# Hybrid decoder layer: the causal mask of the stick-breaking heads, as matrix products or as zeros written by GpSimd

## The chip, the cores and the metric

One core of a Trainium2 chip runs the whole layer. The metric is the device time in microseconds (us) of one execution; several executions are timed and the median is given. One further execution is recorded by the hardware profiler, and all trace times below are of that one.

## The reference

The layer reads 256 tokens of width 1024. One input projection feeds 8 heads of stick-breaking attention and 8 heads of dilated-window softmax attention; both are normalised per head, joined, projected, added to the input, layer-normed, and followed by a SwiGLU feed-forward network (width 2816) with a second layer norm. Only the stick-breaking part is changed:

```python
def stick_breaking_attention(q, k, v):
    ...
        z = jnp.einsum('bhqd,bhkd->bhqk', q_blk, k).astype(jnp.float32) * scale
        mask = key_pos[None, :] < q_pos[:, None]
        log_stay = jnp.where(mask, jax.nn.log_sigmoid(-z), 0.0)
        after = lax.cumsum(log_stay, axis=3, reverse=True) - log_stay
        w = jnp.where(mask, jnp.exp(jax.nn.log_sigmoid(z) + after), 0.0)
        return jnp.einsum('bhqk,bhkd->bhqd', w.astype(v.dtype), v)
```

A query sees only keys strictly before it. Outside of the mask, the softplus of the score counts as zero in the cumulative sum, and the weight is zero.

## The kernel before

Products that need accuracy are made of two fp32r parts, a rounded one ("hi") and the rest ("lo"): `prod` (L223) issues three TensorE products, hi by hi, hi by lo, lo by hi. So every weight must be split before use. `split` (L78) does that with an ACT copy into `whi` and a DVE subtraction into `wlo`. The class `Weights` (L82) loads chunks of 128x2048 over the SP queue into `wraw` and splits them piece by piece, 512 columns at a time.

Heads go in pairs, `j` = 0 to 3 stick-breaking, 4 to 7 dilated. A stick-breaking pair passes these steps:

- `evacuate` (L253) copies a pair's projected queries and keys out of PSUM in hi and lo parts: `padhi` on ACT and `padlo` on DVE for each head, then `oh` on ACT and `ol` on DVE.
- `stick_scores` (L280), step 1, makes the scores, transposed (keys on the partitions): `z0` (128x512: two heads, first block of keys against all 256 queries) and `z1` (128x256: second block of keys against the second block of queries). Two more products with `identb` as weights and the bf16 tile `maskb` (zeros, and -1e30 where a key isn't before its query) add the mask to the four diagonal blocks. Then ACT computes Abs, Exp and Ln into `ab`, DVE completes the softplus (L300, one instruction for each of `z0` and `z1`), rounds it to `sph` (L301) and subtracts for `spl` (L302).
- `stick_weights` (L305), step 2, adds the cumulative sums to the scores with six products (L311), and ACT takes Exp into `w0` and `w1` (L314, L315).
- `values` (L363), step 3, multiplies with the values (L370, L375) and squares; `normalise` (L384), step 4, sums the squares with `blkr` (L388) and scales.

TensorE's order of these steps among the projection's products is laid out by the class `Order` (L408). It keeps a clock, `now`, in its own units. `fill(cost, fn)` first runs every step that is due, then issues one group of projection products and adds its cost to `now`: 0.65 for three 512-column products of the value projection (`v_proj`, L468), 0.33 for three 256-column ones (`qk_proj`, L484). A step that runs adds its own cost, and the next step of its pair falls due its lag later. `LAG_A` (L29) holds the lags from evacuation to step 1, to step 2, to step 3 and to step 4. Step 3 also waits until the value projection is out (`v_at`). The first two pairs are special: their projections come before the loop, and `attend` is called at `now` = 0 with lags 0.65 and 3.1. In the kernel before:

```python
    attend(0, p01[0], 0.65)
    ...
    attend(1, p01[1], 3.1)
    ...
        od.after(lags[0] if lag is None else lag, 1.2 if a_kind else 0.97, step1)
```

Behind them come the value projection of the stick-breaking heads (16 fills, chunks 0 and 1), the query-key projections of pairs 2 and 3, the value projection of the dilated heads, and so on. All eight pieces of chunks 0 and 1 are issued ahead of the first fill: one, then the evacuation of pair 0, two more, the evacuation of pair 1, and five more.

The framework's scheduler may move instructions of an engine past each other by its own estimate of when they are ready. The wrapper `Pinned` (L62) holds the instructions issued through it (`prod`, `split`, `evacuate`) in program order, up to step 1 of pair 1; from there on it is off. ACT's and DVE's instructions of `stick_scores` are not issued through it.

Of the kernel before, what the change touches and what calls it, by code (L numbers as in the profile page):

```python
# [12 lines left out]
BF16 = mybir.dt.bfloat16  # L13
AF = mybir.ActivationFunctionType
ALU = mybir.AluOpType
# [10 lines left out]

PACE = 1.39
LEAD = 5
LAG_A = (5.13, 7.73, 1.37, 1.88)  # L29
LAG_B = (3.34, 5.0, 1.13, 4.28)  # L30
LAG_LN = 5.92
LAG_LN1 = 5.94
# [11 lines left out]
NEG = -1.0e30  # L44
# [3 lines left out]
def decoder_layer(ctx: ExitStack, tc: tile.TileContext, first, x, wqk, wv, wo, wgu, wd,  # L48
                  gmix, lnrows, biases, out):
    nc = tc.nc  # L50
    cst = ctx.enter_context(tc.tile_pool(name="cst", bufs=1))
# [21 lines left out]
    pe, act_e, dve = Pinned(nc.tensor), Pinned(nc.scalar), Pinned(nc.vector)  # L73

    def bank(tag, name):
        return ps.tile([128, 512], F32, tag=tag, name=name)
# [112 lines left out]
    negones = cst.tile([128, 128], F32R, name="negones")  # L189
    negtri = cst.tile([128, 128], F32R, name="negtri")  # L190
    ident = cst.tile([128, 128], F32, name="ident")
    identb = cst.tile([128, 128], BF16, name="identb")
    maskb = cst.tile([128, 128], BF16, name="maskb")
    blkr = cst.tile([128, 128], F32R, name="blkr")
    along, back = [[1, 128]], [[-1, 128]]

    nc.gpsimd.memset(maskb, 0.0)
    nc.gpsimd.affine_select(maskb, maskb, along, ALU.is_gt, NEG, base=0, channel_multiplier=-1)
    nc.gpsimd.memset(ident, 1.0)
    nc.gpsimd.affine_select(ident, ident, back, ALU.is_equal, 0.0, base=0, channel_multiplier=1)  # L200
    nc.gpsimd.tensor_copy(identb, ident)
    nc.gpsimd.memset(negones.bitcast(F32), -1.0)
    nc.gpsimd.affine_select(negtri, negones.bitcast(F32), back, ALU.is_ge, 0.0, base=0, channel_multiplier=1)
    nc.gpsimd.memset(blkr.bitcast(F32), 0.0)
# [18 lines left out]
    def prod(dst, lhs, rhs, start, stop):  # L223

        pe.matmul(dst, lhs[0], rhs[0], start=start, stop=False, skip_group_check=True)
        pe.matmul(dst, lhs[0], rhs[1], start=False, stop=False, skip_group_check=True)
        pe.matmul(dst, lhs[1], rhs[0], start=False, stop=stop, skip_group_check=True)
# [25 lines left out]
    def evacuate(j, p):  # L253

        a_kind = j < 4
        ph, pl = padded[j % 2]
        oh = at.tile([128, S], F32R, tag="oh", name="oh")
        ol = at.tile([128, S], F32R, tag="ol", name="ol")
        qs = slice(0, 256)
        ks = slice(256, 512)  # L260
        pc, oc = (qs, ks) if a_kind else (ks, qs)
        pscale, oscale = (SCALE, 1.0) if a_kind else (1.0, SCALE)
        for h in range(2):
            r = slice(h * 64, h * 64 + 64)
            c = slice(h * 256, h * 256 + 256)
            act_e.activation(ph[r, c], p[r, pc], AF.Copy, scale=pscale)
            dve.scalar_tensor_tensor(pl[r, c], p[r, pc], pscale, ph[r, c],
                                     op0=ALU.mult, op1=ALU.subtract)
        act_e.activation(oh, p[:, oc], AF.Copy, scale=oscale)
        dve.scalar_tensor_tensor(ol, p[:, oc], oscale, oh, op0=ALU.mult, op1=ALU.subtract)  # L270
        return (ph, pl), (oh, ol)

    def heads(t, n):
        return t[:, :2 * n].rearrange("p (h n) -> p h n", h=2)

    def second(t):

        return t.rearrange("p (h n) -> p h n", h=2)[:, :, 128:256]

    def stick_scores(j, pad, plain):  # L280
        ph, pl = pad
        oh, ol = plain
        z0 = bank("big", "z0")
        z1 = bank("sml", "z1")
        prod(z0, (oh[:, 0:128], ol[:, 0:128]), (ph, pl), True, True)
        prod(heads(z1, 128), (oh[:, 128:256], ol[:, 128:256]), (second(ph), second(pl)), True, True)
        mb = maskb[:, None, :].to_broadcast([128, 2, 128])
        z0d = z0.rearrange("p (h n) -> p h n", h=2)
        pe.matmul(z0d[:, :, 0:128], identb, mb, start=False, stop=True, skip_group_check=True)
        pe.matmul(heads(z1, 128), identb, mb, start=False, stop=True, skip_group_check=True)  # L290
        sph = sk.tile([128, 768], F32R, tag="sph", name="sph")
        spl = sk.tile([128, 768], F32R, tag="spl", name="spl")
        ab = at.tile([128, 768], F32, tag="ab", name="ab")
        parts = ((z0, slice(0, 512), 512), (z1, slice(512, 768), 256))
        for z, c, n in parts:
            nc.scalar.activation(ab[:, c], z[:, :n], AF.Abs)
        nc.scalar.activation(ab, ab, AF.Exp, scale=-1.0)
        nc.scalar.activation(ab, ab, AF.Ln, bias=1.0)
        for z, c, n in parts:
            nc.vector.scalar_tensor_tensor(ab[:, c], z[:, :n], 0.0, ab[:, c], op0=ALU.max, op1=ALU.add)  # L300
        nc.vector.tensor_copy(sph, ab)  # L301
        nc.vector.tensor_sub(spl, ab, sph)  # L302
        return z0, z1, sph, spl

    def stick_weights(z0, z1, sph, spl):  # L305
        z0d = z0.rearrange("p (h n) -> p h n", h=2)
        for sp in (sph, spl):
            s1 = sp[:, 512:768]
            for dst, lhs, rhs in ((z0, negtri, sp[:, 0:512]), (z0d[:, :, 128:256], negones, heads(s1, 128)),
                                  (z1[:, :256], negtri, s1)):  # L310
                nc.tensor.matmul(dst, lhs, rhs, start=False, stop=True, skip_group_check=True)  # L311
        w0 = at.tile([128, 512], F32, tag="w0", name="w0")
        w1 = at.tile([128, 256], F32, tag="w1", name="w1")
        nc.scalar.activation(w0, z0, AF.Exp)  # L314
        nc.scalar.activation(w1, z1[:, :256], AF.Exp)  # L315
        return w0, w1

    bias_sb = at.tile([128, 8, 256], F32, name="bias_sb", bufs=1)
# [124 lines left out]
    od = Order()  # L443

    def attend(j, p, lag=None):

        a_kind = j < 4
        pad, plain = evacuate(j, p)
        scores, weigh = (stick_scores, stick_weights) if a_kind else (dilated_scores, dilated_weights)
        lags = LAG_A if a_kind else LAG_B  # L450

        def step1():
            x1 = scores(j, pad, plain)
            Pinned.on = Pinned.on and j == 0

            def step2():
                x2 = weigh(*x1)

                def step3():
                    x3 = values(j, *x2)  # L460
                    od.after(lags[3], 0.43, lambda: normalise(j, *x3))
                od.after(lags[2], 0.68, step3, lambda: v_at.get(j // 4, 1e9) <= od.now)
            od.after(lags[1], 0.9 if a_kind else 0.65, step2)
        od.after(lags[0] if lag is None else lag, 1.2 if a_kind else 0.97, step1)

    vt, v_at = {}, {}

# [16 lines left out]
    def qk_proj(j, c0):  # L484
        w = weights.get(c0)
        p = bank("in", "p_in")
        for half in range(2):
            for kt in range(KT):
                od.fill(0.33, lambda: qk_step(p, w, half, kt, kt == 0))
        weights.free(c0)  # L490
        attend(j, p)


    weights.piece(512)
    attend(0, p01[0], 0.65)
    for _ in range(2):
        weights.piece(512)
# [213 lines left out]
    base = 14 + NFF  # L711
# [117 lines left out]
```

## Time and profile before

| | us |
|---|---|
| median of 3 runs (317.07 to 317.55) | 317.19 |
| the profiled execution | 316.86 |
| its span, first to last instruction | 315.1 |
| TensorE busy in the span | 305.9 |
| VectorE (DVE) busy | 240.6 |
| ScalarE (ACT) busy | 190.7 |
| GpSimd (POOL) busy | 4.1 |

The profiled execution took 1.76 us more than its span, which lie around it, and it is 0.33 us under the median. In the rows below, PE is TensorE's products and PEld its weight loads. Products overlap in the pipeline and the ends shown for them are modelled, so what a product costs is read from one start to the next, not from its duration. A row of the timeline gives its start, its duration, the instruction, how many were merged, and in brackets the engine's idle time before it with what ended it.

### The profile page before, as it was taken

The numbers are of one execution on the slowest core, as the hardware profiler recorded it, in microseconds if no ns is written. First come the engines' busy times: TensorE is split into PE (matmuls) and PEld (weight loads), VectorE is DVE, ScalarE is ACT, GpSimd is POOL, SyncE is SP. The second block draws the span as 40 slices with busy tenths as digits, with TensorE's granted clock in tenths as the row PEclk, the third lists the DMA queues.
The fourth block names the chain that finished last, engine by engine and source line by source line (L and its number), as shares of the span: only waits on it lengthen the run. The fifth ranks groups of instructions, "written<-read, shape, count | busy, mean of one in ns | idle before, by whom it ended". The sixth has DMA issues, their size and how long they took to land.

```text
span 315.1 us, 5440 instructions
## 1 busy us (share of the span) xinstructions
PE 305.9 (97%) x2112; PEld 277.8 (88%) x2112; DVE 240.6 (76%) x465; ACT 190.7 (61%) x406; POOL 4.1 (1%) x22
## 2 busy tenths in 40 slices
PE   8999999999999999999999999999999999999990
PEld 4988898799997778999999999999999988888880
DVE  4778998659897479997646466585597699999765
ACT  5789997777787458666446364473542675565011
POOL 5000000000000000000000000000000000000000
PEclk9999999999999999999999999999999999999998
DMA  7979887297332104789455464563613253630011
GB/s 255 399 301 381 277 283 263 113 358 292 151 137 69 64 2 133 249 294 370 157 189 214 139 226 172 166 235 133 218 50 136 80 188 130 270 135 0 0 67 67
DMA packets 9657, 58.02 MB, mean 184 GB/s; under 512 B 1184, under 2 KB 1440, under 8 KB 3360
## 3 DMA queue, kind: packets, MB, share of 16 engines
q1 hardware_dynamic: 9344, 57.22, 49.8%
q10 hardware_dynamic: 288, 0.46, 0.4%
q8 instruction: 16, 0.26, 0.3%
q14 instruction: 9, 0.07, 0.1%
HBM read 56.63 MB, written 1.05 MB: 183 GB/s over the span
## 4 chain that ended last, share of the span: by engine, by line
PE 94%; DVE 2%; ACT 1%; DMA 1%; issue 0%; DVEq 0%
PE pg L71 40%; PE p_in L71 22%; PE d L71 15%; PE acc L71 7%; PE z L71 2%; PE o L370 1%; PE s L71 1%; PE warm L185 1%; PE z L311 1%; DVE y L563 1%; PE o L375 1%; DVE bst L548 1%; DMA out_h<-y 1%; DVE y L546 1%; PE o L388 1%; PE tr L575 1%
## 5 line engine op out<-in xcount | busy, mean ns | idle before, releaser
L71 DVE TENSOR_TENSOR wlo<-wraw,whi 128x512 fp32r<-128x512 f32 (+2 forms) x194 | 138.0, 739 | 37.9 <-ACT whi L71 37.0
L71 ACT ACTIVATE whi<-wraw 128x512 fp32r<-128x512 f32 (+2 forms) x194 | 121.2, 671 | 58.0 <-PE pg L71 35.2
L71 PE MATMUL pg<-xhi,whi 128*128 128x256 f32 x304 | 85.7, 282 | 0.0
L71 PE MATMUL pg<-xlo,whi 128*128 128x256 f32 x304 | 85.5, 281 | 0.0
L71 PE MATMUL pg<-xhi,wlo 128*128 128x256 f32 x304 | 85.5, 281 | 0.0
L71 PEld LDWEIGHTS pg<-xhi,whi 128*128 128x128 f32 x304 | 57.2, 188 | 0.0
L71 PEld LDWEIGHTS pg<-xlo,whi 128*128 128x128 f32 x304 | 57.2, 188 | 0.0
L71 PEld LDWEIGHTS pg<-xhi,wlo 128*128 128x128 f32 x304 | 57.2, 188 | 0.0
L71 PE MATMUL p_in<-xhi,whi 128*128 128x256 f32 x128 | 36.5, 286 | 0.0
L71 PE MATMUL p_in<-xhi,wlo 128*128 128x256 f32 x128 | 36.3, 283 | 0.0
L71 PE MATMUL p_in<-xlo,whi 128*128 128x256 f32 x128 | 36.1, 282 | 0.0
L71 PE MATMUL d<-whi,s 128*128 128x512 f32 x84 | 26.9, 395 | 0.0
L71 PE MATMUL d<-whi,a 128*128 128x512 f32 (+1 forms) x92 | 25.9, 363 | 0.0
L71 PEld LDWEIGHTS p_in<-xhi,whi 128*128 128x128 f32 x128 | 24.1, 188 | 1.4 <-issue 0.7
L71 PEld LDWEIGHTS p_in<-xlo,whi 128*128 128x128 f32 x128 | 24.1, 188 | 0.2
L71 PEld LDWEIGHTS p_in<-xhi,wlo 128*128 128x128 f32 x128 | 24.1, 188 | 0.1
L71 PEld LDWEIGHTS d<-whi,s 128*128 128x128 f32 x84 | 15.8, 188 | 3.8
L71 PEld LDWEIGHTS d<-whi,a 128*128 128x128 f32 x92 | 16.6, 189 | 2.9
L71 PE MATMUL d<-wlo,a 128*128 128x512 f32 (+1 forms) x46 | 16.7, 363 | 0.0
L71 PE MATMUL d<-wlo,s 128*128 128x512 f32 x42 | 16.6, 395 | 0.0
L71 ACT ACTIVATE s<-slots 128x896 fp32r<-128x896 f32 x6 | 5.7, 953 | 13.4 <-DVE slots L611 13.4
L71 PE MATMUL pg<-wlo,xhi 128*128 128x256 f32 x48 | 13.6, 286 | 0.0
(151 smaller groups left out, 473.7 us busy)
## 6 DMA issues: line engine op xcount, KB each, us to landing
wraw<-in_wgu SPq DMA_DIRECT2D x22, 1024.0 KB, 4.8
wraw<-in_wd SPq DMA_DIRECT2D x11, 1024.0 KB, 4.8
wraw<-in_wqk SPq DMA_DIRECT2D x6, 1024.0 KB, 5.7
wraw<-in_wo SPq DMA_DIRECT2D x4, 1024.0 KB, 4.7
wraw<-in_first SPq DMA_DIRECT2D x8, 384.0 KB, 6.3
wraw<-in_wv SPq DMA_DIRECT2D x3, 1024.0 KB, 5.4
rows<-in_lnrows SPq DMA_DIRECT2D x2, 1024.0 KB, 6.6
wraw<-in_wv SPq DMA_DIRECT2D x2, 512.0 KB, 7.0
```

The source lines that it names most:

```text
L71: return lambda *a, **k: tc.keep_in_program_order(f(*a, **k)) if Pinned.on else f(*a, **k)
L185: nc.tensor.matmul(warm.rearrange("p (r n) -> p r n", r=4), idle, idle[:, None, :].to_broadcast([128, 4, 128]), start=True, stop=True, ski ...
L311: nc.tensor.matmul(dst, lhs, rhs, start=False, stop=True, skip_group_check=True)
L370: nc.tensor.matmul(o[r, 0:256], vt[g, 0][:, c], w0[:, h * 256:h * 256 + 256], start=True, stop=False, skip_group_check=True)
L375: nc.tensor.matmul(o[r, 128:256], vt[g, 1][:, c], w1[:, h * 128:h * 128 + 128], start=False, stop=True, skip_group_check=True)
L388: nc.tensor.matmul(ms, blkr, sq[:, i, :], start=i == 0, stop=i == 1, skip_group_check=True)
L546: nc.vector.scalar_tensor_tensor(y[:, c], res[:, c], scale, acc[i][:, :c.stop - c.start], op0=ALU.mult, op1=ALU.add)
L548: nc.vector.bn_stats(st[:, i, :], y[:, c])
L563: nc.vector.scalar_tensor_tensor(dst[:, c], y[:, c], r[:, 3:4], b[:, c], op0=ALU.mult, op1=ALU.add)
L575: nc.tensor.transpose(p[:, i * 128:i * 128 + 128], h[:, kt * 128:kt * 128 + 128], ident)
```

## The change

The two mask products of each stick-breaking pair go, and with them `maskb` and `identb` and the three GpSimd instructions that built these. In their place a function `causal` lets GpSimd write zeros into the diagonal blocks (128 columns of each of two heads, 256 columns an instruction) of `ab` after the softplus, and of `w0` and `w1` after the exponential: four instructions for a pair, 16 in all. The second and third lag of `LAG_A` are longer, and the cost that `Order` counts for step 1 is 1.05 in place of 1.2.

```diff
-LAG_A = (5.13, 7.73, 1.37, 1.88)
+LAG_A = (5.13, 8.4, 2.1, 1.88)
...
-    identb = cst.tile([128, 128], BF16, name="identb")
-    maskb = cst.tile([128, 128], BF16, name="maskb")
...
-    nc.gpsimd.memset(maskb, 0.0)
-    nc.gpsimd.affine_select(maskb, maskb, along, ALU.is_gt, NEG, base=0, channel_multiplier=-1)
...
-    nc.gpsimd.tensor_copy(identb, ident)
...
+    def causal(t, n):
+
+        d = t.rearrange("p (h n) -> p h n", h=2)[:, :, 0:128]
+        nc.gpsimd.affine_select(d, d, [[0, 2], [1, 128]], ALU.is_gt, 0.0, base=0, channel_multiplier=-1)
+
     def stick_scores(j, pad, plain):
...
-        mb = maskb[:, None, :].to_broadcast([128, 2, 128])
-        z0d = z0.rearrange("p (h n) -> p h n", h=2)
-        pe.matmul(z0d[:, :, 0:128], identb, mb, start=False, stop=True, skip_group_check=True)
-        pe.matmul(heads(z1, 128), identb, mb, start=False, stop=True, skip_group_check=True)
...
         for z, c, n in parts:
             nc.vector.scalar_tensor_tensor(ab[:, c], z[:, :n], 0.0, ab[:, c], op0=ALU.max, op1=ALU.add)
+            causal(ab[:, c], n)
         nc.vector.tensor_copy(sph, ab)
         nc.vector.tensor_sub(spl, ab, sph)
...
         nc.scalar.activation(w0, z0, AF.Exp)
+        causal(w0, 512)
         nc.scalar.activation(w1, z1[:, :256], AF.Exp)
+        causal(w1, 256)
...
-        od.after(lags[0] if lag is None else lag, 1.2 if a_kind else 0.97, step1)
+        od.after(lags[0] if lag is None else lag, 1.05 if a_kind else 0.97, step1)
```

## Rows read from the trace of the kernel before

**Rows 1.** Page, part 1: engine, busy time (share of the span), instructions.
```profile
PE 305.9 (97%) x2112; PEld 277.8 (88%) x2112; DVE 240.6 (76%) x465; ACT 190.7 (61%) x406; POOL 4.1 (1%) x22
```

**Rows 2.** All waits of PE: who waited for whom, us in total, times, longest.
```profile
PE warm L185 <- DVE idle L182: 1.1, 1, 1.1
PE o L370 <- ACT w L359: 0.2, 1, 0.2
```

**Rows 3.** Timeline of PE, 18.8 to 23 us: step 1 of pairs 0 and 1.
```profile
18.86 0.28 PE L71 MATMUL z<-padhi,ol 128*128 128x256 f32 x1
18.98 0.39 PE L71 MATMUL z<-maskb,identb 128*128 128x256 bf16 x2
...
19.45 0.39 PE L71 MATMUL p_in<-wlo,xhi 128*128 128x512 f32 x1
...
20.60 0.47 PE L71 MATMUL z<-padhi,oh 128*128 128x512 f32 x1
...
21.91 0.48 PE L71 MATMUL p_in<-whi,xhi 128*128 128x512 f32 x1
...
22.69 0.39 PE L71 MATMUL p_in<-whi,xhi 128*128 128x512 f32 x1
```

**Rows 4.** Timeline of PE, the same passage from 256 to 512 columns without masks.
```profile
29.09 0.28 PE L311 MATMUL z<-spl,negtri 128*128 128x256 f32 x1
...
29.44 0.39 PE L71 MATMUL p_in<-wlo,xhi 128*128 128x512 f32 x1
```

**Rows 5.** Timeline of ACT, then of DVE, 18 to 27 us: evacuation of pair 1, splits.
```profile
18.78 0.38 ACT L71 ACTIVATE padhi<-p_in 64x256 fp32r<-64x256 f32 x1 [0.90 <-DVE padlo L71]
19.30 0.87 ACT L296 ACTIVATE ab<-z 128x512 f32<-128x512 f32 x2
20.06 0.39 ACT L71 ACTIVATE oh<-p_in 128x256 fp32r<-128x256 f32 x1
20.32 2.72 ACT L71 ACTIVATE whi<-wraw 128x512 fp32r<-128x512 f32 x5
...
20.48 0.42 DVE L71 SCALAR_TENSOR_TENSOR ol<-p_in,oh 128x256 fp32r<-128x256 f32 x1 [0.86 <-ACT oh L71]
21.00 3.10 DVE L71 TENSOR_TENSOR wlo<-wraw,whi 128x512 fp32r<-128x512 f32 x5
...
26.56 0.68 DVE L71 TENSOR_TENSOR wlo<-wraw,whi 128x512 fp32r<-128x512 f32 x1
```

**Rows 6.** Timeline of PE around step 3: pairs 0 and 1 together, then pair 3.
```profile
34.24 0.28 PE L71 MATMUL p_in<-xhi,wlo 128*128 128x256 f32 x1
...
36.12 0.28 PE L71 MATMUL p_in<-xlo,whi 128*128 128x256 f32 x1
...
64.64 0.28 PE L71 MATMUL p_in<-xhi,wlo 128*128 128x256 f32 x1
...
65.87 0.28 PE L71 MATMUL p_in<-xlo,whi 128*128 128x256 f32 x1
```

**Rows 7.** Timeline of POOL, whole span, three of its 22 instructions.
```profile
1.65 0.20 POOL L202 MEMSET negones<- 128x128 f32 x1
...
2.04 0.29 POOL L203 TENSOR_SCALAR_AFFINE_SELECT negtri<-negones 128x128 fp32r<-128x128 f32 x1
...
4.21 0.52 POOL L248 MEMSET padlo<- 128x512 f32 x1
```

**Rows 8.** Stretch table (busy us of PE, PEld, DVE, ACT, POOL), then DVE and PE timelines.
```profile
24.00:39.00 15.00, 15.00 (x98) 12.86 (x97) 13.96 (x25) 14.89 (x32) 0.00 (x0) 1.00 0.89 332
...
36.32 0.92 DVE L381 TENSOR_TENSOR sqh<-sq,sqh 128x256 fp32r<-128x256 f32 x2
...
37.41 0.40 PE L388 MATMUL o<-sqh,blkr 128*128 128x256 f32 x2
```

**Rows 9.** Timelines of DVE and of PE: pair 2, end of step 1, step 2.
```profile
53.73 0.96 DVE L302 TENSOR_TENSOR spl<-ab,sph 128x768 fp32r<-128x768 f32 x1
...
57.20 0.41 PE L311 MATMUL z<-spl,negtri 128*128 128x512 f32 x1
```

More of the change, by code (lines that the diff above doesn't have):

```diff
@@ L191, in decoder_layer @@
     ident = cst.tile([128, 128], F32, name="ident")
-    identb = cst.tile([128, 128], BF16, name="identb")
-    maskb = cst.tile([128, 128], BF16, name="maskb")
     blkr = cst.tile([128, 128], F32R, name="blkr")
-    along, back = [[1, 128]], [[-1, 128]]
-    nc.gpsimd.memset(maskb, 0.0)
-    nc.gpsimd.affine_select(maskb, maskb, along, ALU.is_gt, NEG, base=0, channel_multiplier=-1)
+    back = [[-1, 128]]
     nc.gpsimd.memset(ident, 1.0)
     nc.gpsimd.affine_select(ident, ident, back, ALU.is_equal, 0.0, base=0, channel_multiplier=1)
-    nc.gpsimd.tensor_copy(identb, ident)
     nc.gpsimd.memset(negones.bitcast(F32), -1.0)
```

## The prediction, made before the changed kernel was run

> **What bounds the kernel now.** I read the page's busy shares first: TensorE is busy 305.9 of 315.1 us, every other engine 76% or less [rows 1]. Then the waits of TensorE alone: in the whole span there are two, 1.1 us for the warm-up at the start and 0.2 us for a dilated pair [rows 2]. So in the stage of the stick-breaking heads, from 17 to 68 us, TensorE's products follow one another without a wait, and a change is worth what it takes out of TensorE's sequence or puts in as a wait. The third view is the timeline around each changed instruction, where I look for two things: the cost of a mask product from start to start, and how soon before its use each operand is ready.
>
> **What the masks cost.** From the last 256-column product of pair 0's scores (18.86) to the second 512-column product behind the masks (19.45) are 0.59 us [rows 3]. The same passage without masks is 29.09 to 29.44, 0.35 us [rows 4]. So the two masks of a pair cost 0.24 us (four pairs show 0.23 to 0.24), and removing eight products takes 4 x 0.24 = 0.96 us out of TensorE's sequence. If nothing else moved, that would be the gain: 0.3%.
>
> **What the new cost and lags do to the order of pair 1.** The order can be worked out from the planner's numbers. Before: the first fill ends at 0.65, step 1 of pair 0 runs and takes `now` to 1.85, two fills take it to 3.15; this is past 3.1, so step 1 of pair 1 runs ahead of the fourth fill. The trace agrees: its first product starts at 20.60, the fourth fill at 21.91 [rows 3]. After: step 1 of pair 0 counts 1.05, `now` is 1.70, after two fills 3.00. That is not 3.1. So a third fill is issued, and step 1 of pair 1 follows the fourth fill in all. Both go through the pinned wrapper, so the scheduler can't swap them back.
>
> The fourth fill multiplies with piece 3 of chunk 0, and this piece is late. ACT's and DVE's orders are pinned too: the piece stands behind the evacuation of pair 1. DVE makes `ol` from 20.48, then five splits from 21.00 [rows 5], and the first of them is this piece. One split takes 0.68 [rows 5], so it ends at 21.68. In the kernel before, the fourth fill's second product, the first that reads `wlo`, starts 0.32 after 21.91 (as 19.45 does behind its masks), at 22.23: 0.55 us of cover. After, without the first pair's masks, the fourth fill comes at 20.60 - 0.24 = 20.36, its second product at 20.59. The cover is gone.
>
> How early can the piece be? With the mask of `z0` gone, ACT's two Abs need not wait for it: they start at 19.30 where `padhi` ended at 18.78 + 0.38 = 19.16 [rows 5]. Neighbours on ACT overlap by some 0.1, so Abs gains 0.1 to 0.25, and `oh`, `ol` and the split gain the same: the piece ends at 21.43 to 21.58. TensorE follows an operand by about 0.15 (`oh` ends at 20.45, the product starts at 20.60 [rows 3, 5]). So the second product starts at 21.58 to 21.73, and with two products of 0.23 behind it step 1 of pair 1 starts at 22.04 to 22.19, though it would be due at 20.36 + 0.69 = 21.05: a new stall of 1.0 to 1.15 us. If the scheduler places the Abs after the pieces instead, `oh` comes some 0.4 earlier, and the stall is 0.7; if nothing on ACT gets earlier it is 1.25.
>
> The sum at a common point, the start of the fifth fill: before 22.69 [rows 3]. After: 22.04 to 22.19, plus three products of 0.235 and three of 0.12 (1.06), so 23.10 to 23.25. That is +0.41 to +0.56, I take +0.48, with both masks of pairs 0 and 1 already taken out (bounds with the two other placements +0.1 to +0.65). The masks of pairs 2 and 3 bring -0.48. These two cancel.
>
> **Steps 2 and 3.** By the same arithmetic, after the change steps 2 of both pairs stand one or two fills later, and step 3 of pair 0 comes one fill behind the value projection, with step 3 of pair 1 four fills later. Before, both step 3 came together. From the last product ahead to the second behind, the two together take 36.12 - 34.24 = 1.88, less two pitches of 0.12: 1.64. Pair 3 alone takes 65.87 - 64.64 = 1.23, so 0.99 [rows 6]. Two apart cost 1.98: +0.34 (range 0.2 to 0.4, since the matrix switches form four times and not twice).
>
> **GpSimd's own work.** No row shows a 256-column select. One of 128 columns took 0.29; a memset grows from 0.20 (128 columns) to 0.52 (512), 0.11 per 128 [rows 7]. So an instruction takes between 0.29 and 0.58; I take 0.40, from the memset's slope. For the softplus the first select hides under DVE's second instruction; the second delays `sph` by about 0.40 plus two handovers of 0.15, 0.7 in all; the weights are delayed by the same 0.7. Step 2 gets one fill more (0.69) and 0.67 more of lag, step 3 0.73 more. In pair 2 `spl` ended at 54.69 and was used at 57.20, 2.5 us of cover [rows 9], and so no stall there. In pairs 0 and 1 DVE and ACT have no slack: 13.96 and 14.89 of 15 us busy [rows 8]. There the new stall is 0 to 0.8; I take 0, since the fills added equal the delay and the scheduler may fill gaps with other products from there on. Below zero it doesn't go: nothing waits now. The three instructions that GpSimd saves at the start (about 0.8 us) cost and give nothing: its last one ended long before the first evacuation.
>
> Behind a waiting `sph` stand, on DVE, the splits of later weights and, from 36.32, the squares that step 4 needs. The squares ended at 37.24, and TensorE used the first at 37.41 [rows 8]; that first one ended about 36.8, 0.6 ahead.
>
> The rule that speaks against this change: the Trainium skill, "SBUF — State Buffer", section "SBUF: two separate sides", says that DVE and GpSimd share one pair of ports by an exclusive lock, held for the whole instruction by whichever starts first, for DVE instructions with two SBUF inputs as well. No row here shows it: GpSimd's last instruction comes just before DVE's first subtraction. By that rule each select among the splits would hold DVE up, or be held up; without it the sum stays as it is, and with it the result is the second rival below.
>
> **The sum.** +0.48 - 0.48 + 0.34 = +0.34 us, so 317.2 against the profiled 316.86, and against the median of 317.19 about 317.5. Its own range is -0.18 (0.1 - 0.48 + 0.2) to +1.37 (0.65 - 0.48 + 0.4 + 0.8): 317.0 to 318.6.
>
> **The rivals.** *The stall doesn't come* (0.20): the fourth fill and step 1 of pair 1 stay swapped, or the piece is split earlier than the pinned order says. Then the masks' 0.96 come out, less 0.34 for the separated step 3: 316.6; without that 316.2. For it: from 24 us on the scheduler does move products. Against it: up to 24 us the trace follows the program's order exactly.
>
> *DVE is held up by GpSimd* (0.25), which ends slower: DVE is busy without a gap from 25 us to the squares of step 4, so a delay there goes through to TensorE's products of step 4. Eight selects of pairs 0 and 1 at 0.40 make 3.2 us if every one holds DVE up. It decides once the delay exceeds the 0.6 us of cover. With half of the eight, 1.6 us, the stall is 1.0 on top of the forecast: 318.5; with all it would be 2.6, 320.1.
>
> *The forecast* has the rest, 0.55.
>
> **How the numbers follow.** A measurement can tell about 0.2%, 0.63 us, from no change: 316.56 to 317.82. Of the forecast's 0.55, most (0.42) lies inside and 0.13 above. Of the first rival 0.13 is faster and 0.07 inside. Of the second 0.20 is slower and 0.05 inside. That makes faster 0.13, same 0.54, slower 0.33. For 8 in 10 the range reaches from 316.5 (cuts off half of the first rival) to 318.6 (cuts off a part of the second).
>
> **What would show it.** Right: in the trace after, TensorE waits near 21 us for a `wlo` or `whi` (none is listed now), the fourth fill stands ahead of pair 1's scores, the fifth fill starts near 23.2, and the two step 3 stand apart. The fifth fill starting near 22.2 would show the first rival; TensorE waiting for `sqh`, `sph` or `spl` between 28 and 40 us, with GpSimd's selects or DVE's splits longer than their 0.3 to 0.6 and 0.68, the second. Wrong altogether would be a difference that arises behind 68 us, where no instruction of the change stands.

## The result and the profile after

The changed kernel takes 318.89 us (median of 5 runs, 318.6 to 319.4) against 317.32 us before: 1.57 us more, ratio 1.0052 (95% interval 1.0041 to 1.0064). It is slower by more than the 0.2% that can be told from no change, and above the predicted range (316.5 to 318.6). Its profiled execution took 319.1 us, its span is 317.4 us. In this document a median is that of all runs of a kernel, and a ratio leaves out the few runs far above the kernel's fastest (one of the five of e5 below, 773 us against 318.3 to 319.0).

The page of after, part 1, to be read against [rows 1]; then the one line among the waits of PE that [rows 2] doesn't have (who waited for whom, us in total, times, longest):

```profile
PE 306.6 (97%) x2104; PEld 278.0 (88%) x2104; DVE 241.6 (76%) x465; ACT 191.1 (60%) x406; POOL 13.2 (4%) x35
...
PE p_in L71 <- DVE ol L71: 1.5, 1, 1.5
...
```

Eight products fewer (2104 against 2112), GpSimd busy for 13.2 us in place of 4.1, and one new wait of TensorE, 1.5 us, of nearly the size of the loss. It would be easy to stop here; the budget below, and a run without that wait, show that this agreement is chance.

**Where the time arises.** The two profiles don't begin alike: the first product of the value projection starts 0.64 us later after (17.82) than before (17.18). The change puts no instruction ahead of that point, it only takes three of GpSimd's away; in kernels that differ from before in a planner's number alone (below) the same start shifts by 0.67 and 0.71. Over all fourteen profiles it lies between 17.18 and 17.90, with masks and without, and the profile of before happens to be the earliest. So each shift below is taken less its own profile's start shift. Timeline of PE after, first products of the sixth fill of the value projection, of the 13th fill of pair 2's query-key chunk, and of the first and the 13th fill of pair 5's:

```profile
25.19 0.39 PE L71 MATMUL p_in<-whi,xhi 128*128 128x512 f32 x1
...
41.66 0.28 PE L71 MATMUL p_in<-xhi,whi 128*128 128x256 f32 x1
...
72.12 0.29 PE L71 MATMUL p_in<-xhi,whi 128*128 128x256 f32 x1
...
77.80 0.28 PE L71 MATMUL p_in<-xhi,whi 128*128 128x256 f32 x1
```

| up to | start before | start after | shift less 0.64 | arises in the stretch |
|---|---|---|---|---|
| sixth fill (steps 1 of pairs 0 and 1) | 23.38 | 25.19 | +1.17 | +1.17 |
| pair 2's 13th fill (steps 2 to 4 of pairs 0 and 1) | 39.33 | 41.66 | +1.69 | +0.52 |
| pair 5's first fill (pairs 2 and 3) | 70.26 | 72.12 | +1.22 | -0.47 |
| pair 5's 13th fill (scores of pair 4) | 75.66 | 77.80 | +1.50 | +0.28 |
| end of the span | 315.13 | 317.36 | +1.59 | +0.09 |

The sum, +1.59, agrees with the medians' 1.57. Each of the first four stretches has its own cause; the last 0.09 isn't explained, and most kernels below show about as much there.

**Steps 1 of pairs 0 and 1: +1.17.** Timeline of PE after, against [rows 3]:

```profile
20.80 0.40 PE L71 MATMUL p_in<-whi,xlo 128*128 128x512 f32 x1
22.66 0.70 PE L71 MATMUL p_in<-whi,xhi 128*128 128x512 f32 x2 [1.46 <-DVE ol L71]
...
24.14 0.40 PE L71 MATMUL z<-padhi,oh 128*128 128x512 f32 x1
```

The fourth fill now stands ahead of pair 1's scores, as worked out, and with it the products of the fifth. From 20.80 to 22.66 are 1.86 us for a product of 0.23: a stall of 1.63, not the 1.0 to 1.15 predicted. The reason stands on ACT, then DVE (against [rows 5]):

```profile
19.49 0.60 ACT L292 ACTIVATE ab<-z 128x512 f32<-128x512 f32 x1 [0.97 <-PE z L71]
20.11 0.38 ACT L71 ACTIVATE padhi<-p_in 64x256 fp32r<-64x256 f32 x1
20.52 0.38 ACT L292 ACTIVATE ab<-z 128x256 f32<-128x256 f32 x1
20.93 0.84 ACT L293 ACTIVATE ab<-ab 128x768 f32<-128x768 f32 x1
21.69 0.36 ACT L71 ACTIVATE oh<-p_in 128x256 fp32r<-128x256 f32 x1
21.95 2.70 ACT L71 ACTIVATE whi<-wraw 128x512 fp32r<-128x512 f32 x5
...
22.08 0.42 DVE L71 SCALAR_TENSOR_TENSOR ol<-p_in,oh 128x256 fp32r<-128x256 f32 x1 [1.13 <-ACT oh L71]
22.60 2.50 DVE L71 TENSOR_TENSOR wlo<-wraw,whi 128x512 fp32r<-128x512 f32 x4
```

Before, ACT made pair 1's second `padhi`, then both Abs, then `oh` at 20.06. After, the Abs of `z0` comes ahead of that `padhi`, and the second Abs and the Exp of pair 0 ahead of `oh`, which starts at 21.69: 1.63 later, 0.99 of it beyond the start shift. `ol` and every piece of the weights behind it are late by as much. The profile puts TensorE's wait down to `ol`; what the waiting product reads is the fourth fill's `whi`, which ACT makes right behind `oh`, and which is the first of the five from 21.95.

**Steps 2 to 4 of pairs 0 and 1: +0.52.** Timeline of PE, step 3 of pair 0, then of pair 1, and step 4 of both, against [rows 6]:

```profile
34.99 0.27 PE L71 MATMUL p_in<-xhi,wlo 128*128 128x256 f32 x1
...
36.22 0.28 PE L71 MATMUL p_in<-xlo,whi 128*128 128x256 f32 x1
...
37.39 0.28 PE L71 MATMUL p_in<-xhi,wlo 128*128 128x256 f32 x1
...
38.40 0.57 PE L387 MATMUL o<-sqh,blkr 128*128 128x256 f32 x2
...
38.92 0.28 PE L71 MATMUL p_in<-xlo,whi 128*128 128x256 f32 x1
...
40.60 0.51 PE L387 MATMUL o<-sqh,blkr 128*128 128x256 f32 x2
40.95 0.28 PE L71 MATMUL p_in<-xhi,whi 128*128 128x256 f32 x1
```

The two step 3 stand apart. Pair 0's takes 36.22 - 34.99 = 1.23, less two pitches 0.99, as pair 3's did before. Pair 1's takes 38.92 - 37.39 = 1.53; less the two products of step 4 that follow on it (0.24, as from 37.41 to 37.65 before) and two pitches it is 1.05. Together 2.04 against 1.64: +0.40. And the second step 4 takes 40.95 - 40.60 = 0.35 in place of 0.24. Such prices of a change of form (the step from products of one shape to those of another) are read from start to start, like a wait. That is +0.51, the whole of this stretch: in this kernel TensorE waits for nothing of GpSimd in pairs 0 and 1.

**Pairs 2 and 3: -0.47**, the four mask products, predicted as -0.48. (The other kernels without these masks show -0.31 to -0.48 here.)

**Scores of pair 4: +0.28.** PE before (the first two rows), then PE, ACT and DVE after. Step 4 of pair 3 (`mh` on ACT is one of its instructions) stands among pair 4's evacuation:

```profile
74.30 0.28 PE L71 MATMUL s<-padlo,oh 128*128 128x256 f32 x1
74.42 0.35 PE L71 MATMUL s<-padhi,ol 128*128 128x256 f32 x1
...
76.16 0.28 PE L71 MATMUL s<-padlo,oh 128*128 128x256 f32 x1
76.51 0.39 PE L71 MATMUL s<-padhi,ol 128*128 128x256 f32 x1
...
73.96 0.42 ACT L71 ACTIVATE mh<-sq 128x256 fp32r<-128x256 f32 x1
...
75.45 0.39 ACT L71 ACTIVATE oh<-p_in 128x256 fp32r<-128x256 f32 x1
...
76.03 0.42 DVE L71 SCALAR_TENSOR_TENSOR ol<-p_in,oh 128x256 fp32r<-128x256 f32 x1
```

The product with `ol` starts 0.35 after its forerunner and not 0.12: `ol` itself only starts at 76.03. This stall is 0.23 of the 0.28; the product after it follows 0.23 behind (76.51 to 76.74) and not 0.19.

### The profile page after: what moved, and what is told of

It reads as the page before. It is cut to its first block, busy times and chain, and to the rows that moved or that the text cites. A ratio compares the mean times of both kernels' runs of the same rounds, so it can differ in the third digit from the quotient of the medians.

```text
span 317.4 us, 5442 instructions
## 1 busy us (share of the span) xinstructions
PE 306.6 (97%) x2104; PEld 278.0 (88%) x2104; DVE 241.6 (76%) x465; ACT 191.1 (60%) x406; POOL 13.2 (4%) x35
## 3 DMA queue, kind: packets, MB, share of 16 engines
HBM read 56.63 MB, written 1.05 MB: 182 GB/s over the span
## 4 chain that ended last, share of the span: by engine, by line
PE 92%; DVE 3%; ACT 2%; DMA 1%; issue 0%; DVEq 0%
PE pg L71 40%; PE p_in L71 20%; PE d L71 15%; PE acc L71 7%; PE o L369 1%; PE warm L185 1%; PE s L71 1%; PE z L71 1%; PE z L308 1%; DVE y L562 1%; PE o L387 1%; PE o L374 1%; DVE bst L547 1%; DMA out_h<-y 1%; DVE y L545 1%; PE tr L574 1%
## 5 line engine op out<-in xcount | busy, mean ns | idle before, releaser
L71 PE MATMUL p_in<-whi,xhi 128*128 128x512 f32 x32 | 12.6, 400 | 1.5 <-DVE ol L71 1.5
```

Source lines behind the costliest of these rows:

```text
L71: return lambda *a, **k: tc.keep_in_program_order(f(*a, **k)) if Pinned.on else f(*a, **k)
```

## The experiments

Four theories came from this comparison. *ACT's order*: without the masks the scheduler draws pair 0's Abs and Exp ahead of pair 1's evacuation. *The swap*: the cost 1.05 puts the fourth fill ahead of pair 1's scores. *The selects*: GpSimd's work delays `sph`, `spl` and the weights, here hidden behind the first stall. *The lags*: the longer lags, with the cost 1.05, separate step 3, and they push step 4 of pair 3 into pair 4's evacuation. (The quoted texts were written before the runs, and some call theories by letters of their own; the words beside a letter say which is meant.) All ratios are against the kernel before, run beside them (317.1 to 317.3 us). The table gives for each the shift, less that of its start, at the points of the table above.

| kernel | median us | ratio (95% interval) | sixth fill | pair 2's 13th | pair 5's first | pair 5's 13th | end |
|---|---|---|---|---|---|---|---|
| after | 318.89 | 1.0052 (1.0041 to 1.0064) | +1.17 | +1.69 | +1.22 | +1.50 | +1.59 |
| e1 after, cost 1.2 | 318.56 | 1.0039 (1.0026 to 1.0052) | +0.68 | +1.23 | +0.83 | +1.11 | +1.17 |
| e2 before, cost 1.05 | 317.78 | 1.0014 (1.0005 to 1.0023) | +0.33 | +0.41 | +0.41 | +0.41 | +0.49 |
| e3 before, new lags | 317.90 | 1.0015 (1.0006 to 1.0024) | 0.00 | +0.01 | +0.06 | +0.34 | +0.44 |
| e4 before, 16 selects | 318.64 | 1.0040 (1.0027 to 1.0052) | -0.02 | +0.94 | +1.24 | +1.24 | +1.23 |
| e5 after, Abs held | 318.82 | 1.0045 (1.0032 to 1.0059) | -0.24 | +1.47 | +1.07 | +1.35 | +1.41 |
| e6 after, Abs held, cost 1.2 | 318.00 | 1.0023 (1.0014 to 1.0032) | -0.56 | +0.84 | +0.39 | +0.66 | +0.68 |
| e8 after, ACT's order and cost of before | 317.76 | 1.0017 (1.0008 to 1.0026) | -0.35 | +0.57 | +0.09 | +0.38 | +0.49 |
| e9 e8, both step 3 together | 317.29 | 1.0001 (0.9992 to 1.0010) | -0.39 | +0.15 | -0.26 | +0.02 | +0.12 |
| e10 before, selects on `ab` | 317.49 | 1.0006 (0.9997 to 1.0015) | +0.01 | +0.37 | +0.37 | +0.37 | +0.48 |
| e11 before, selects on `w0`, `w1` | 317.66 | 1.0016 (1.0007 to 1.0024) | -0.02 | +0.22 | +0.52 | +0.52 | +0.57 |
| e12 e9, shorter lags for pairs 2 and 3 | 317.04 | 0.9992 (0.9983 to 1.0001) | -0.37 | +0.12 | -0.19 | -0.08 | +0.02 |
| e13 before, selects in pairs 2 and 3 alone | 316.83 | 0.9996 (0.9987 to 1.0005) | -0.02 | -0.03 | -0.44 | -0.33 | -0.23 |

The last column and the difference of the medians agree within 0.35 us in all of them; differences of that size are not read.

### Undo the swap in the changed kernel

```diff
-        od.after(lags[0] if lag is None else lag, 1.05 if a_kind else 0.97, step1)
+        od.after(lags[0] if lag is None else lag, 1.2 if a_kind else 0.97, step1)
```

> The changed kernel with the planner's cost of step 1 back at 1.2, and nothing else. By the planner's numbers step 1 of pair 1 then stands ahead of the fourth fill again, and both step 3 stand together again. Theory A (the order on ACT: without the masks pair 0's Abs and Exp stand ahead of pair 1's oh, which ends 1.0 us later relative to the start of the value projection, and TensorE waits behind it): the wait stays, now in front of pair 1's scores, about 1.2 us; with 0.96 of masks gone the time is 317.4 to 317.9. Theory B (only the swapped order of fill 4 and pair 1's scores on TensorE): the wait goes, 316.2 to 316.6. Theory C (DVE held up by GpSimd): stays near 318.9.

The stall stayed, and the time lies above the 317.4 to 317.9 expected from ACT's order alone. Waits of PE in e1, behind the start-up's and up to pair 4:

```profile
PE z L71 <- ACT oh L71: 1.0, 1, 1.0
PE z L308 <- DVE spl L299: 0.3, 1, 0.3
```

Pair 1's scores stand ahead of the fourth fill again, and now they themselves wait 1.0 us for `oh`, which ACT again makes behind the Exp. So the swap is not the main cause of the new stall. Both step 3 stand together again (36.30 and 37.01), so the second stretch loses nothing to them; a second wait, for `spl`, comes to light in their place. The product with it comes 0.42 late and loses 0.1 to the next, nearly the whole of that stretch's +0.55.

### Make the swap in the kernel before

```diff
-        od.after(lags[0] if lag is None else lag, 1.2 if a_kind else 0.97, step1)
+        od.after(lags[0] if lag is None else lag, 1.05 if a_kind else 0.97, step1)
```

> The kernel before, masks and lags as they were, with the planner's cost of step 1 at 1.05: fill 4 then stands ahead of pair 1's scores on TensorE, while on ACT pair 0's two Abs still stand behind both padhi and Exp behind oh, as before. Theory A alone: no late oh, so little wait; theory B: fill 4's second product is due at 20.8 and its wlo ends at 21.7, a wait of about 0.9 in the trace near 21 us and 318.1 to 318.4. Theory C: 317.3, no change.

With the masks in place ACT keeps its old order, and the swap alone costs +0.33 at the sixth fill and nothing behind it. The time is below the 318.1 to 318.4 expected from the swapped order. The wait for the late piece, PE in e2:

```profile
21.77 0.70 PE L71 MATMUL p_in<-whi,xhi 128*128 128x512 f32 x2 [0.30 <-DVE ol L71]
```

By the prediction's arithmetic without its masks the cost should be about 0.96 (+0.48, with the 0.48 of pairs 0 and 1 put back). The scheduler fills part of the gap with the fifth fill's first product, the second of the x2 here as at 22.66 after: TensorE's order around the swap was not as firm as I took it.

### The new lags in the kernel before

```diff
-LAG_A = (5.13, 7.73, 1.37, 1.88)
+LAG_A = (5.13, 8.4, 2.1, 1.88)
```

> The kernel before with the two longer lags alone. By the planner's numbers step 2 of pairs 0 and 1 comes one fill later, both step 3 stay together, and pairs 2 and 3 shift by one to four fills. All theories: no change, 317.0 to 317.5; a change over 0.5 us would mean that the lags cost by themselves what is laid to ACT's order or to GpSimd.

A miss: 0.2% slower, with nothing else changed. Up to pair 5's first fill nothing moves; then pair 4's scores wait for `ol`, as after. PE and DVE of e3:

```profile
75.03 0.28 PE L71 MATMUL s<-padlo,oh 128*128 128x256 f32 x1
75.39 0.39 PE L71 MATMUL s<-padhi,ol 128*128 128x256 f32 x1
...
74.91 0.42 DVE L71 SCALAR_TENSOR_TENSOR ol<-p_in,oh 128x256 fp32r<-128x256 f32 x1
```

The lags need no select and no missing mask to cost 0.28 there. Both step 3 stay together, as in e2: neither the lags nor the cost separates them alone. By the planner's arithmetic step 4 of pair 3 stands six fills ahead of pair 4's evacuation before and one fill ahead with the new lags.

### The selects in the kernel before

The masks stay as products, and the selects (the function `causal` of the change) come on top, so the mask is applied twice:

```diff
...
+            causal(ab[:, c], n)
...
+        causal(w0, 512)
...
+        causal(w1, 256)
```

> The kernel before with its masks, its lags and its cost of step 1, and the 16 selects of GpSimd added (they write zeros where zeros stand already): the cost of the selects alone, with the order of fill 4, of Abs and of both step 3 as before. Theory A: nothing or little, 317.2 to 317.5, since TensorE's order is that of before. Theory C: 0.5 to 1.3 us, 317.7 to 318.5, with DVE instructions beside a select longer than alone (a split over 0.75 us, the rounding of sph over 0.6) and a wait of TensorE for spl or w.

The selects alone cost 1.2 us by the profile and 1.4 by the medians, at or above the most that was expected (1.3): +0.94 in steps 2 and 3 of pairs 0 and 1, +0.30 at step 3 of pair 3. Two waits of PE behind 24 us that before didn't have (for pair 3's weights, for pair 1's `sph`), and the instructions of DVE around pair 1's softplus in e4:

```profile
PE o L377 <- POOL w L282: 0.2, 1, 0.2
...
PE z L316 <- DVE sph L306: 0.2, 1, 0.2
...
31.75 0.74 DVE L306 CAST sph<-ab 128x768 fp32r<-128x768 f32 x1 [0.30 <-POOL ab L282]
32.42 0.89 DVE L71 TENSOR_TENSOR wlo<-wraw,whi 128x512 fp32r<-128x512 f32 x1
```

DVE waits 0.30 for GpSimd, and its own instructions stretch beside a select: `sph` 0.74 where it takes 0.55 to 0.56 alone, the next `wlo` 0.89 in place of 0.68. TensorE's first product with `sph` comes late by more than the wait listed: it follows 0.60 behind the product ahead of it and not 0.23.

### The selects taken apart

e10 keeps only the calls on `ab`, e11 only those on the weights; the diffs are against e4.

```diff
-        causal(w0, 512)
...
-        causal(w1, 256)
```

```diff
-            causal(ab[:, c], n)
```

> The kernel before (masks as products, lags and cost unchanged) with only the two selects on `ab` of each pair: GpSimd writes zeros into the softplus sums, eight instructions in all, and nothing into the weights. Theory: of the 1.2 us that all sixteen selects cost in the kernel before, the larger part is the DVE chain of steps 1 and 2 (sph waits for GpSimd, then the splits of the weights stand behind it), so about +0.6 to +0.9 us against before, 317.9 to 318.2, most of it between the fifth fill and the first query-key chunk. Rival (the cost is the contention beside DVE's splits, whichever tile is written): half of 1.2, and the same as the selects on the weights alone, 317.8 each.

> The kernel before with only the two selects on `w0` and `w1` of each pair, nothing on `ab`. Theory: the weights are ready 0.7 to 1 us later, which step 3 has cover for in pairs 0 to 2 (it waits for the value projection), and not in pair 3, so +0.3 to +0.5 us, 317.5 to 317.7, most of it at pair 3 near 66 us. Rival (contention beside DVE's splits): +0.6, 317.8, spread over pairs 0 and 1.

Neither alone is worth half of the 1.2: the medians are +0.17 (an interval that holds no change) and +0.34 us, and up to pair 2's 13th fill the shifts are +0.37 and +0.22, against +0.94 for both. The surplus of both over the sum of the two is 0.35 there, 0.2 by the profiles' ends and 0.9 by the medians, so its size is open. The division that I expected (most of it in `ab`) isn't there. A reading that fits the surplus in pairs 0 and 1: the late `sph` of pair 1 meets the selects on pair 0's weights, so that the two delays don't merely add. One part of it can be seen: in e4 these selects stretch pair 1's `sph` to 0.74, in e10, without them, it takes 0.56, and its first product follows after 0.41 and not 0.60. Pair 3's +0.30 comes from the weights alone, as expected. How the rest of the surplus arises stays open.

### Hold pair 0's Abs behind pair 1's evacuation

In the changed kernel pair 0's Abs are queued behind pair 1's `oh`; e6 has the cost 1.2 besides.

```diff
...
-        act_e.activation(oh, p[:, oc], AF.Copy, scale=oscale)
+        copied[j] = act_e.activation(oh, p[:, oc], AF.Copy, scale=oscale)
...
-        for z, c, n in parts:
-            nc.scalar.activation(ab[:, c], z[:, :n], AF.Abs)
+        with tc.issue_after(copied[1 if j == 0 else j].ins):
+            for z, c, n in parts:
+                nc.scalar.activation(ab[:, c], z[:, :n], AF.Abs)
```

> The changed kernel with pair 0's two Abs queued on ACT behind pair 1's oh; TensorE's planner numbers as changed. Theory A: oh of pair 1 ends near 20.0 (on the scale of the trace of before), the fourth piece near 21.3, the wait at fill 4 falls from 1.5 to 0.5 to 0.8 us, and the time by about 0.7 to 1.0 us, to 317.9 to 318.2. Theory B: the wait at fill 4 is that of the forecast, 1.0 less 0.4: about 317.9 too, but then the changed kernel's own wait of 1.5 is not explained. Theory C: 318.9.

> Both of the above: the changed kernel, step 1 counted at 1.2 and pair 0's Abs behind pair 1's oh. Theories A and B together: no wait near 21 us is left, both step 3 stand together, and the masks' 0.96 us come out whole: 316.2 to 316.5, faster than both kernels. Theory C: still near 318.9, or at least above 317.3.

ACT of e5, pair 1's `oh`:

```profile
19.95 0.38 ACT L71 ACTIVATE oh<-p_in 128x256 fp32r<-128x256 f32 x1 [0.49 <-DVE padlo L71]
```

This decides the first stretch: the +1.17 at the sixth fill becomes -0.24 with the swap and -0.56 without it. The stall near 21 us is ACT's order, and with it gone the masks of pairs 0 and 1 show as the gain they were worked out to be. But the times miss what ACT's order and the swap promised (317.9 to 318.2, and 316.2 to 316.5) and agree with the theory of the selects. The total of e5 stays where after's is: +1.71 now arises in steps 2 to 4, in place of +0.52. Of it, about 0.3 stand at pair 1's first product with `sph` and about 0.5 among pair 1's products with the weights, which follow late; the rest is mostly changes of form, since the steps of the two pairs now stand among one another. That the first stall had given DVE and ACT the time to get ahead is read from this; in the changed kernel itself no product of steps 2 and 3 waits. Holding the Abs until `oh` also makes that softplus later than it need be (e8 below, which holds it less, loses 0.92 here). In e6 it arises too, +1.40, on top of a better start, and the total falls by 0.9.

### ACT's order of before, then step 3 together, then shorter lags

e8 puts pair 0's Abs behind pair 1's second `padhi` and its Exp behind pair 1's `oh`, which is ACT's order of before, with the cost 1.2 as in e1. e9 changes one more line: by the planner both step 3 fall due together in e8 too, but in its trace they stand apart, and released 0.7 units later they stand together; e12 changes one more.

```diff
...
-        for z, c, n in parts:
-            nc.scalar.activation(ab[:, c], z[:, :n], AF.Abs)
-        nc.scalar.activation(ab, ab, AF.Exp, scale=-1.0)
+        with tc.issue_after(second_pad[max(j, 1)].ins):
+            for z, c, n in parts:
+                nc.scalar.activation(ab[:, c], z[:, :n], AF.Abs)
+        with tc.issue_after(copied[max(j, 1)].ins):
+            nc.scalar.activation(ab, ab, AF.Exp, scale=-1.0)
...
-        v_at[g] = od.now + 1.2
+        v_at[g] = od.now + (1.9 if g == 0 else 1.2)
...
-        lags = LAG_A if a_kind else LAG_B
+        lags = (LAG_A if j < 2 else (5.13, 7.73, 1.7, 1.88)) if a_kind else LAG_B
```

> The changed kernel with step 1 counted at 1.2 and ACT's order of pair 0 and 1 held as in the kernel before: pair 0's two Abs behind pair 1's second padhi, pair 0's Exp behind pair 1's oh. Theory A (the loss is ACT's order and the swapped fill): no wait near 21 us, the fifth fill 0.4 to 0.5 us earlier than before (counted from the start of the value projection), and since Abs is not late either, step 2 and 3 of pairs 0 and 1 lose only what two separated step 3 cost, 0.3 to 0.5: 316.6 to 317.1. Theory C (the selects make DVE's softplus late, and TensorE pays at steps 2 and 3 whatever ACT's order): the loss between the fifth fill and the projection of pair 3 stays near 1.4 us, 317.7 to 318.1.

> The kernel above, with step 3 of pairs 0 and 1 released 0.7 units of the planner later, so that both stand together on TensorE as in the kernel before. Theory A: the separated step 3 are saved, 0.3 to 0.5 us less than the run above, 316.3 to 316.8, faster than the kernel before. Theory C: TensorE waits for spl or w of pair 1, or the gain is below 0.2 us.

> The kernel of the last run of this line (selects, no mask products, ACT's order as before, both step 3 together behind a later release) with the lags of pairs 2 and 3 back near the old ones: 7.73 to step 2 and 1.7 to step 3, so that step 4 of pair 3 comes one fill later than before instead of five. If the longer lags delay pair 4's evacuation: pair 4's scores wait no more, 0.3 to 0.4 us less than that run, so 316.9, faster than before by 0.1%, with the shift between the fourth query-key chunk and the scores of pair 4 near 0. If the selects of pairs 2 and 3 need the longer lags: a wait of TensorE for `w0` or `sph` between 54 and 67 us in its place, and 317.3 or more.

ACT's order and the cost bring 1.1 us of the 1.57 (318.89 to 317.76), and the sixth fill comes 0.35 early; but the total is the 317.7 to 318.1 of the theory of the selects, not the 316.6 to 317.1 of the other, since +0.92 still arise in steps 2 to 4. The two step 3 together bring 0.47 more (317.76 to 317.29; 0.42 by the shifts), as was expected of them: about the +0.51 that the same separation cost by the rows of after. The shorter lags bring 0.25 by the medians and 0.10 by the profiles' ends, less than is read here; what the rows do show is that pair 4's product with `ol` follows after 0.15 and no longer 0.35:

```profile
74.17 0.28 PE L71 MATMUL s<-padlo,oh 128*128 128x256 f32 x1
74.32 0.39 PE L71 MATMUL s<-padhi,ol 128*128 128x256 f32 x1
```

What is left is the selects' own price, in step 2 of pair 1. PE in e9, then the `sph` on DVE that the first product with it reads:

```profile
31.57 0.40 PE L71 MATMUL p_in<-whi,xlo 128*128 128x512 f32 x1
31.94 0.50 PE L311 MATMUL z<-sph,negtri 128*128 128x512 f32 x1
32.28 0.28 PE L311 MATMUL z<-sph,negones 128*128 128x256 f32 x1
...
33.35 0.28 PE L71 MATMUL p_in<-xlo,whi 128*128 128x256 f32 x1
33.62 0.50 PE L311 MATMUL z<-spl,negtri 128*128 128x512 f32 x1
33.96 0.28 PE L311 MATMUL z<-spl,negones 128*128 128x256 f32 x1
...
31.15 0.74 DVE L301 CAST sph<-ab 128x768 fp32r<-128x768 f32 x1 [0.30 <-POOL ab L279]
```

The first products with `sph` and with `spl` come 0.14 and 0.15 late and take 0.34 and not 0.23 to the next: 0.5 us in all, just the masks' 0.48 of these two pairs. So of the gain of 0.96 that was worked out, e12 shows 0.37 up to the sixth fill and 0.31 over pairs 2 and 3; 0.49 go back to the selects, 0.1 at pair 4's scores, and the time of before is reached again, not clearly beaten.

### The selects where they have cover

In the kernel before, pairs 2 and 3 alone use selects in place of the mask products, with the lags of e12 for these pairs.

```diff
-        pe.matmul(z0d[:, :, 0:128], identb, mb, start=False, stop=True, skip_group_check=True)
-        pe.matmul(heads(z1, 128), identb, mb, start=False, stop=True, skip_group_check=True)
+        if j < 2:
+            pe.matmul(z0d[:, :, 0:128], identb, mb, start=False, stop=True, skip_group_check=True)
+            pe.matmul(heads(z1, 128), identb, mb, start=False, stop=True, skip_group_check=True)
...
+            if j > 1:
+                causal(ab[:, c], n)
...
+        if select:
+            causal(w0, 512)
...
+        if select:
+            causal(w1, 256)
...
-        lags = LAG_A if a_kind else LAG_B
+        lags = (LAG_A if j < 2 else (5.13, 7.73, 1.7, 1.88)) if a_kind else LAG_B
```

> The kernel before with GpSimd's selects in place of the mask products in pairs 2 and 3 alone (where the products that a select delays have cover), the lags of these two pairs 7.73 to step 2 and 1.7 to step 3; pairs 0 and 1, the cost of step 1 and the lag of 3.1 stay as before. If the loss of the change lies in pairs 0 and 1, in the separated step 3 and in the long lags, nothing is left here but the four mask products saved, 0.48, less some 0.1 that step 4 of pair 3 costs nearer to pair 4's evacuation: 316.9 against 317.3, the shift at the fifth fill and at the second query-key chunk 0, and -0.3 to -0.5 at pair 4's chunk. Rival: the selects cost TensorE as much in pairs 2 and 3 as in pairs 0 and 1 (0.2 to 0.3 a pair), and the time is that of before within 0.1%.

The profile shows what was expected, no shift in pairs 0 and 1 (-0.02 and -0.03), -0.44 over pairs 2 and 3, +0.11 given back at pair 4's scores. The median is 0.26 under before (316.83 against 317.09), but the interval of the ratio, 0.9987 to 1.0005, holds no change too: a gain of this size isn't established. No kernel run here clearly beats before.

## Why the prediction was wrong

**What bounds the kernel, the masks' cost: right.** Every loss that was found is a wait or a change of form in TensorE's sequence. The masks are worth about 0.24 us a pair: -0.47 over pairs 2 and 3 after, -0.44 in e13 (-0.31 to -0.48 in the rest), and -0.35 to -0.56 at the sixth fill where ACT's order is mended and the swap undone.

**The order of pair 1: the swap right, the size wrong, and this is the step that failed.** The planner's arithmetic of the order held. The term +0.48 (bounds +0.1 to +0.65) measured +1.17, compared at the sixth fill, since the fifth fill's products moved ahead. The failing sentence is that without the mask the Abs gain 0.1 to 0.25 "and `oh`, `ol` and the split gain the same". It took ACT's order as fixed and let the Abs move only in time. The evacuations are pinned among one another, the Abs and the Exp are not; [rows 5] had shown it, for the program issues pair 0's Abs behind all eight pieces, and there they stand at 19.30 ahead of pair 1's `oh`. Freed of the mask products they became ready earlier in the scheduler's estimate, and it put them in front: the freeing that I counted as a gain of 0.1 to 0.25 is a loss of 0.99 at `oh`. The text weighed one other placement, the Abs after the pieces; the third, ahead of `oh` and with the Exp, was not weighed. That the masks are the trigger is shown by exclusion: with the masks kept and one other part of the change put in (the cost in e2, the lags in e3, the selects in e4) `oh` isn't late, with the masks gone and the cost as before (e1) it is. A kernel with pair 0's masks taken out and nothing else was not run. That it is an estimate of readiness inside the scheduler that turns is read from the new order; the scheduler's numbers are not on record. The swap itself was priced too high: alone it costs 0.33 (e2) where the arithmetic gives 0.96, and with the Abs held the stretch is -0.24 (e5), below the lower bound of +0.1, since products of the fifth fill move into the gap.

**Step 3 apart: right, the size low, 0.34 (0.2 to 0.4) against 0.51.** The part from rows 6 measured 0.40, the upper bound; the changes of form at step 4 were left out.

**GpSimd: the length right only alone, the stall 0 by luck.** A select takes 0.41 alone (estimate 0.40), but nine of the sixteen after took 0.55 to 1.12, beside DVE. The stall taken as 0 is 0 after, but not because fills and lags cover it: the stall near 21 us did. In the kernel with that stall removed the selects cost 0.5 us in step 2 of pair 1 (e9); in the kernel before, with the short lags, 1.2 (e4). So the second rival, to which the prediction gave 0.25, was right in kind: DVE is held up by GpSimd. Its place was step 2 and not step 4, and in the changed kernel it is masked.

**Behind 68 us: wrong.** That "no instruction of the change stands" there is so, but its lags reach there: +0.28 at pair 4's scores, shown alone by e3. I followed the moved step 4 of pairs 0 and 1 and not that of pair 3, which runs into another pair's evacuation on ACT and DVE.

Of the signs that the prediction named, those for right came (a wait near 21 us, the fourth fill ahead of pair 1's scores, both step 3 apart), and so did the one for wrong, a difference behind 68 us: the signs named where something would happen and not how much it would cost. The first rival, that the stall doesn't come, is out. Of the 1.25 us between the forecast's +0.34 and the budget's +1.59, 0.69 lie in the first stretch (1.17 for 0.48), 0.18 in steps 2 to 4 (0.52 for 0.34), 0.01 in pairs 2 and 3, and 0.37 behind them, where 0 was expected.

## What to carry to other kernels

Taking an operation off one engine also changes when its consumers look ready, and a scheduler may then move them ahead of something more urgent on another engine: check whether the consumers are pinned, and weigh each order they could take. When the wait that you find equals the loss, remove it before you believe it: here the kernel without the wait was as slow, since the wait covered the next delay. A longer lag isn't free because nothing waits where it was put in (e3: 0.01 us in pairs 0 and 1, 0.28 behind pair 3); follow the last pair that it moves to whatever runs behind it.

## What the runs showed of the hardware

GpSimd and DVE lengthen one another. Timelines of POOL and DVE after: pair 0's selects on `ab` (the first beside the end of DVE's softplus instruction, the second with DVE idle), then both of pair 1's on `ab` and both of pair 0's on the weights:

```profile
26.38 0.41 POOL L278 TENSOR_SCALAR_AFFINE_SELECT ab<-ab 128x256 f32<-128x256 f32 x1 [22.12 <-DVE ab L296]
...
27.18 0.56 DVE L298 CAST sph<-ab 128x768 fp32r<-128x768 f32 x1 [0.54 <-POOL ab L278]
...
30.48 0.41 POOL L278 TENSOR_SCALAR_AFFINE_SELECT ab<-ab 128x256 f32<-128x256 f32 x1 [3.33 <-DVE ab L296]
...
30.66 0.77 DVE L71 TENSOR_TENSOR wlo<-wraw,whi 128x512 fp32r<-128x512 f32 x1
30.84 0.86 POOL L278 TENSOR_SCALAR_AFFINE_SELECT ab<-ab 128x256 f32<-128x256 f32 x1
...
32.45 0.70 POOL L278 TENSOR_SCALAR_AFFINE_SELECT w<-w 128x256 f32<-128x256 f32 x1 [0.76 <-ACT w L311]
...
32.80 1.16 DVE L299 TENSOR_TENSOR spl<-ab,sph 128x768 fp32r<-128x768 f32 x1
33.11 1.12 POOL L278 TENSOR_SCALAR_AFFINE_SELECT w<-w 128x256 f32<-128x256 f32 x1
```

A select of 256 columns takes 0.41 us by itself, and the same beside the end of the softplus instructions (DVE, 25.62 to 26.63), one of whose inputs lies in PSUM; it takes 0.86 beside a split and 1.12 beside the subtraction for `spl`. The profile's spans of GpSimd are rough, but both long ones end 0.27 after the DVE instruction beside them (31.70 against 31.43, 34.23 against 33.96), whatever that one's length: the select waits it out. In the other direction `wlo` grew from 0.68 to 0.77 and `spl` from 0.95 to 1.16 where a select was under way as they began (those from 30.48 and from 32.45), each by some 0.14 less than the select had still to run. This agrees with the Trainium skill, "SBUF — State Buffer", section "SBUF: two separate sides", by which the two engines take their shared ports in turn for whole instructions, DVE's with two SBUF inputs included. `sph`, with one SBUF input, grew too in e4, from 0.56 to 0.74; the same section of the Trainium skill counts DVE's instructions in a two-port mode in. That `sph` runs in such a mode isn't shown, but it does 768 columns in 0.56 where `spl` takes 0.95.

And the wait of `sph` for GpSimd shows as idle time of DVE, 0.54 behind pair 0's two selects and 0.30 behind pair 1's. It is the selects' own time and hardly a handover: `sph` starts 0.03 to 0.04 behind the end of the second select (27.18 against 27.14, 31.73 against 31.70). Without the selects it starts 0.03 behind the softplus instruction, so they delay pair 0's `sph` by 0.5, where the prediction, with two handovers of 0.15, took 0.7.
